# A hybrid diffusion layer: late adaLN vectors as weighted sums on VectorE, gates spread by a transfer through DRAM

## The chip, the cores and the metric

The kernel runs on one core of one Trainium2 chip. The metric is the device time of one execution in microseconds (us), the median over several runs. A core has TensorE (PE in the profile, its weight loads as PEld), VectorE (DVE), ScalarE (ACT), GpSimd (POOL) and SyncE (SP, which here only issues transfers), each with an instruction queue of its own that is worked off in order; they wait for each other by semaphores.

## The reference, cut to what matters

One step of one trunk layer for 128 context tokens and 512 latent tokens, D = 1024 channels. Every token is modulated by vectors computed from a condition: `c_ctx` for the context tokens, `c` for the latent ones.

```python
def adaln(cond, w_mod, b_mod):
    m = jax.nn.silu(cond) @ w_mod + b_mod            # w_mod: 1024 x 6144
    return jnp.split(m[..., None, :], 6, axis=-1)
...
sh1, sc1, g1, sh2, sc2, g2 = adaln(c, w_mod[l], b_mod[l])      # and the same with c_ctx
h = rmsnorm(xs, norm1_g[l]) * (1.0 + sc1) + sh1
y, _ = token_mixer(h, *mix_w, pos_lat, ctx)
xs = xs + g1 * y
h = rmsnorm(xs, norm2_g[l]) * (1.0 + sc2) + sh2
xs = xs + g2 * conv_ffn(h, w_up[l], conv_w[l], conv_b[l], w_down[l])
```

`token_mixer` projects `h` to queries, keys, values and gates, runs attention and a bidirectional retention, projects each branch (`w_att_o`, `w_ret_o`), merges them by sigmoid gates and projects by `w_out`. `conv_ffn` is an up projection, a width-3 convolution, a gate and a down projection. `sh1` and `sc1` are needed at the start; the change is about the other four vectors, called late here: `sc2` and `sh2`, needed ahead of the second norm, and the gates `g1` and `g2`, needed at the two residual additions. Each is 1024 numbers for each of the two conditions.

## The kernel before, in words

The 640 tokens are five tiles (NT) of 128. Products with weights are done as three fp32r products of split halves (`mm3`: high by high, high by low, low by high): a weight chunk is loaded on SP (`w_raw`, L133, two buffers), its high half is a copy on ScalarE (L144) and its low half a subtraction on VectorE (L149), eight half tiles of 128x1024 (`wh`) in turn. PE runs through its program in order:

1. The start: `sc1`, `sh1`, the first norm, keys and values, queries, attention.
2. Stage A, 261 to 327 us: 16 half-columns of `w_att_o` (`b_col`, L194 to L196: 24 products of 128x320 each, five banks). VectorE evacuates each with one instruction (L794), and after every second one a transfer on GpSimd stores the result (L796).
3. The groups, 327 to about 430 us: `a_group` over 512 columns of `w_in` for the retention's k, q and v (RK, RQ, RV), five tiles by two halves of 12 products of 128x512 (L156 to L158); the second half of the inner dimension has a weight chunk of its own, so one chunk is due every 14 to 16 us. Rotary embedding of each tile of k and q: two products on GpSimd (L840), then two instructions on VectorE (L842, L843).
4. Retention, then `w_ret_o` in units whose parts are added up by accumulating transfers (`f1.s`), then the out projection, 659 to 735 us (`wo_a`, evacuated by L1239 with the first gate), and the MLP in seven-product units, whose sums keep VectorE busy.

The late vectors are computed in fillers. `mod_rest` is a generator, advanced by one step at each `yield` of stage A (scale and shift) and of the groups (the gates). For each half vector it loads 2 MB of `w_mod` (L248), and TensorE multiplies: 8 blocks of 128 inner rows by 4 column groups, each product with the condition, 32 columns wide, as weights (L256). Four products side by side write to partitions 0, 32, 64 and 96. A copy to SBUF (L259, VectorE) and one product with a selecting constant (L264) turn the row into columns, channel by partition, and `put_vec` adds the bias.

A gate is used along the free dimension, so `gate_rows` spreads it again to all 128 partitions: for each condition and half four f32 products of the column, broadcast, with the identity (L274) and a copy on ScalarE (L276). That happens ahead of the fourth tile of the out projection's first half, and again between the out projection and the first MLP group.

Which instruction of one engine stands before which is decided when the program is built; the lists below show it.

## Time and profile before

| | |
|---|---|
| median of 3 runs | 1170.83 us (1170.36 to 1171.75) |
| profiled execution: span from first to last instruction | 1169.8 us; its own time isn't given apart from the span |
| granted TensorE clock in it | 0.998 |
| PE busy | 1143.2 us, 98% |
| PE weight loads | 1030.1 us, 88% |
| VectorE busy | 772.8 us, 66% |
| ScalarE busy | 591.5 us, 51% |
| GpSimd busy | 180.8 us, 15% |
| transfers | 145.85 MB, mean 125 GB/s |

A row of the timeline gives start and duration in us, engine, line, operation, the tile written, the tiles read, the shape, a count, and in brackets how long the engine was idle before and who released it. Products on PE overlap, so what one costs is the distance between starts, not the duration. In the names of tiles the last number only counts; `mm3.mm` and `aux3.aux` are PSUM banks, `weights.wh` split weights, `weights.raw` loaded ones.

### The profile page before, as it was taken

How to read it: one execution, taken by the hardware profiler on the slowest of the kernel's cores; microseconds unless marked ns; L12 is line 12 of the kernel's file. 1: busy time of each engine (PE TensorE's matmuls, PEld its weight loads, DVE VectorE, ACT ScalarE, POOL GpSimd, SP SyncE). 2: the span in 40 equal slices, each digit the busy share in tenths (PEclk: the TensorE clock that was granted, in tenths of full speed). 3: DMA queues.
4: the chain of work that ended last, by engine and by line, in shares of the span. 5: the costliest groups of instructions: out<-in, count | busy, mean ns of one | idle time of the engine just before them, and what ended most of it. 6: DMA issues, size and time to landing. Idle time of an engine off the chain costs nothing.

```text
span 1169.8 us, 18399 instructions
## 1 busy us (share of the span) xinstructions
PE 1143.2 (98%) x7269; PEld 1030.1 (88%) x7269; DVE 772.8 (66%) x1433; ACT 591.5 (51%) x1087; POOL 180.8 (15%) x194
## 2 busy tenths in 40 slices
PE   5999999999999999999999999999999999999996
PEld 4788899999988888888999988999899999899995
DVE  4666977765233526463757739969767688588888
ACT  5355656552132325452435526667657466565463
POOL 0042200000012200033002123002112111121012
PEclk9999999999999999999999999999999999999999
DMA  9742111116754522111217976445666657566543
GB/s 306 244 136 72 38 36 37 37 35 217 261 175 171 176 76 76 37 37 36 71 38 148 267 110 200 110 83 124 153 132 134 143 136 168 127 117 153 136 110 125
DMA packets 135848, 145.85 MB, mean 125 GB/s; under 512 B 26561, under 2 KB 101393, under 8 KB 135761
## 3 DMA queue, kind: packets, MB, share of 16 engines
q1 hardware_dynamic: 106576, 113.49, 30.1%
...
q14 instruction: 31, 0.25, 0.1%
...
## 4 chain that ended last, share of the span: by engine, by line
PE 80%; DVE 8%; ACT 5%; issue 3%; DMA 2%; POOL 1%; ACTq 0%; DVEq 0%; POOLq 0%
DMA f1.s.11_5326<-spill.u2.2_2889 1%; DMA f1.s.13_5328<-spill.u2.2_2889 1%; DVE x1.u1.1_6460 L1440 1%; DMA weights.raw.414_10840<-in_w_down 0%; POOL f0.s.5_3528 L955 0%; DMA const.u2.2_72<-in_b_mod 0%; DVE x1.u1.1_6460 L1489 0%; DVE x1.u1.1_6460 L1452 0%; ACT acts.u1.1_91 L1104 0%; DVE gt.gt0.5_7309 L1388 0%; DVE weights.raw.395_10492 L1537 0%; DVE x1.u1.1_6460 L1447 0%; DVE acts.u2.2_92 L414 0%; PE mm1.mm.11_295 L158 0%; PE mm7.mm.42_9455 L1559 0%
## 5 line engine op out<-in xcount | busy, mean ns | idle before, releaser
L796 POOL DMA_DIRECT2D spill.u2.2_2889<-f1.s.1_1161 x1 | 0.6, 588 | 130.2 <-DVE mod.u4.4_2848 L587 130.2
L1573 DVE TENSOR_TENSOR t7.u4.4_6978<-t7.u4.4_6978,const.u1.1_70 128x322 f32<-128x322 f32 x10 | 5.0, 496 | 11.8 <-ACT const.u1.1_70 L1572 11.8
L1085 POOL DMA_DIRECT2D weights.wh.164_5980<-weights.raw.156_5913 x1 | 1.3, 1347 | 69.6 <-DVE f1.s.9_5324 L1125 69.6
L892 DVE SCALAR_TENSOR_TENSOR ret2.u1.1_4325<-ret2.u1.1_4325,const.u13.13_88 64x128 f32<-64x128 f32 x24 | 6.8, 339 | 6.6 <-ACT ret2.u1.1_4325 L885 6.5
L894 DVE SCALAR_TENSOR_TENSOR ret2.u1.1_4325<-ret2.u1.1_4325,const.u13.13_88 64x128 f32<-64x128 f32 x24 | 6.6, 386 | 4.8 <-ACT ret2.u1.1_4325 L887 4.8
L842 DVE TENSOR_TENSOR ret.u5.5_3531<-ret.u5.5_3531,ret.u1.1_3524 128x512 f32<-128x512 f32 x5 | 3.5, 692 | 9.4 <-POOL ret.r2k.8_3709 L840 3.3
L842 DVE TENSOR_TENSOR ret.u4.4_3530<-ret.u4.4_3530,ret.u1.1_3524 128x512 f32<-128x512 f32 x5 | 3.5, 692 | 9.0 <-POOL ret.r2k.11_3889 L840 4.7
L566 POOL TENSOR_TENSOR p1.u1.1_605<-p1.u3.3_609,p1q.u1.1_599 128x512 f32<-128x512 f32 x1 | 1.3, 1310 | 43.9 <-DMA p1.u4.4_611<-in_cache_k 43.9
L149 DVE TENSOR_TENSOR weights.wh.108_4359<-weights.raw.106_4356,weights.wh.107_4358 128x1024 fp32r<-128x1024 f32 x1 | 1.2, 1224 | 10.3 <-ACT weights.wh.107_4358 L144 10.3
L144 ACT CAST weights.wh.112_4514<-weights.raw.111_4512 128x1024 fp32r<-128x1024 f32 x1 | 1.1, 1050 | 13.2 <-PE mm3.mm.36_4223 L157 13.2
L411 ACT CAST acts.u1.1_91<-f0.s.2_105 128x640 fp32r<-128x640 f32 x4 | 2.9, 728 | 9.5 <-DVE f0.s.2_105 L409 9.5
L259 DVE COPY mod2.wr.9_4315<-aux3.aux.15_4282 128x128 f32<-128x128 f32 x1 | 0.3, 291 | 10.9 <-PE aux3.aux.15_4282 L256 10.9
L428 PE MATMUL aux1.aux.1_135<-const.u1.1_70,const.u2.2_72 80*128 80x80 f32 x1 | 0.4, 365 | 7.0 <-DMA const.u2.2_72<-in_b_mod 7.0
L955 POOL TENSOR_TENSOR f0.s.5_3528<-f0.s.5_3528,ret2.ny20.13_4911 128x512 f32<-128x512 f32 x5 | 6.0, 1236 | 8.0 <-DVE ret2.ny20.13_4911 L219 8.0
L535 ACT ACTIVATE f0.s.3_711<-f0.s.3_711,p1q.ny20.11_879 128x128 f32<-128x128 f32 x20 | 6.0, 388 | 2.5 <-DVE p1q.ny20.11_879 L217 2.5
L144 ACT CAST weights.wh.67_3362<-weights.raw.66_3360 128x1024 fp32r<-128x1024 f32 x1 | 1.0, 1045 | 11.5 <-PE mm3.mm.8_3141 L195 11.5
L144 ACT CAST weights.wh.77_3617<-weights.raw.76_3615 128x1024 fp32r<-128x1024 f32 x1 | 1.0, 1045 | 11.5 <-PE mm3.mm.16_3454 L195 11.5
L144 ACT CAST weights.wh.72_3542<-weights.raw.71_3540 128x1024 fp32r<-128x1024 f32 x1 | 1.0, 1045 | 11.4 <-PE mm3.mm.12_3298 L195 11.4
L1451 DVE TENSOR_TENSOR x1.u1.1_6460<-x1.u1.1_6460,gate.u1.1_6447 128x512 f32<-128x512 f32 x10 | 6.8, 686 | 0.0
L144 ACT CAST weights.wh.92_3979<-weights.raw.91_3977 128x1024 fp32r<-128x1024 f32 x1 | 1.0, 1047 | 11.2 <-PE mm3.mm.26_3760 L157 11.2
L861 POOL MEMSET ret2.u2.2_4326<- 128x512 f32 x1 | 0.5, 525 | 38.9 <-PE aux3.aux.15_4282 L256 38.9
L1484 POOL TENSOR_TENSOR x1.u1.1_6460<-x1.u1.1_6460,weights.raw.422_11041 128x512 f32<-128x512 f32 x3 | 4.9, 1649 | 10.2 <-ACT x1.tm.112_11054 L1457 7.4
...
## 6 DMA issues: line engine op xcount, KB each, us to landing
spill.u1.1_2888<-x1.u1.1_6460 POOLq DMA_DIRECT2D x5, 512.0 KB, 3.6
xin.u1.1_103<-in_x_sample SPq DMA_DIRECT2D x4, 512.0 KB, 4.7
p0.u5.5_120<-in_w_mod SPq DMA_DIRECT2D x2, 1024.0 KB, 10.2
p0.u6.6_126<-in_w_mod SPq DMA_DIRECT2D x2, 1024.0 KB, 15.2
p0.u7.7_129<-in_w_mod SPq DMA_DIRECT2D x2, 1024.0 KB, 12.1
mod.wm.6_2916<-in_w_mod SPq DMA_DIRECT2D x1, 2048.0 KB
mod.wm.8_3069<-in_w_mod SPq DMA_DIRECT2D x1, 2048.0 KB, 8.5
mod.wm.10_3226<-in_w_mod SPq DMA_DIRECT2D x1, 2048.0 KB, 8.7
```

What stands on the lines that cost most here:

```text
L144: nc.scalar.copy(hi, rv)
L411: nc.scalar.copy(hT[0][:, k, :], xk)
L535: nc.scalar.activation(x[:, j], x[:, j], AF.Copy, scale=rstd[:, j:j + 1])
L566: nc.gpsimd.tensor_mul(ct, r2[:, :, 0, :], gqk[:, i:i + 1, :].to_broadcast([P, 4, P]))
L842: V.tensor_mul(z, z, r1[:, t, 0:1, :].to_broadcast([P, 8, 64]))
L892: V.scalar_tensor_tensor(Ss[0:64, hh, st + 1, j], Ss[0:64, hh, st, j], cdsel[0:64, h:h + 1], Ss[0:64, hh, st + 1, j], op0=ALU.mult, op1=AL ...
L894: V.scalar_tensor_tensor(Ss[64:128, hh, 2 - st, j], Ss[64:128, hh, 3 - st, j], cdsel[64:128, h:h + 1], Ss[64:128, hh, 2 - st, j], op0=ALU. ...
L955: nc.gpsimd.tensor_mul(ov, ov, rso[:, 4 * t:4 * t + 4].unsqueeze(2).to_broadcast([P, 4, P]))
L1440: V.tensor_add(x1[:, t, gs], x1[:, t, gs], down_mul(ps, t, c0))
L1451: V.tensor_mul(x1[:, t, gs], x1[:, t, gs], gb[:, t == 0, gs])
L1484: eng.tensor_mul(x, x, fg[:, c0:c0 + 512])
L1573: V.tensor_sub(u[1][:, hi_u], u[1][:, hi_u], u3[i])
```

## The change

The products of the condition with `w_mod` leave PE. The four late vectors now go through one generator that runs through stage A and the groups. For each vector it loads 8 row blocks of 128x1024 (512 KB each, three buffers); for each block and condition, VectorE adds the block times the condition's number of that row, a scalar by partition, to an accumulator of 128x1024 (the first block's sum is a scaled copy on ScalarE). What is left, the sum over the 128 partitions, is one `fold` for each vector: four f32 products of 512 columns with ones as weights, 32 columns wide, one for each column group. The row goes to SBUF on ScalarE; scale and shift then become columns by four small products, two halves at once. A gate's bias is added before the fold by two accumulating transfers onto partition 0 of the accumulator; its row is halved, stored to DRAM (`gd`), and later loaded with one transfer that repeats it to all partitions (`gate_load`, 1 MB), so that `gate_rows` is gone, with the vectors `gvec`. The generator is advanced at two of three yields of stage A, and once or twice at each of the groups' yields. Of the diff, an unused helper that goes and the old `gate_rows`, printed above, are left out.

```diff
+    def put_vec(kind, i, pv):
+        def parts(x):
+            return x.rearrange("p (h q) c -> p h q c", h=2)
+
+        k4 = [P, 2, 4, 2]
+        bias = cv[:, {"sc": 8, "sh": 7}[kind], :].rearrange("p (h q) -> p h q", h=2).unsqueeze(3).to_broadcast(k4)
+        dst = parts((avec if kind == "sc" else shvec)[i])
         V.tensor_add(dst, pv, bias)
         if kind == "sc":
-            V.scalar_tensor_tensor(dst, dst, 1.0, cv[:, 2 + i, k0:k0 + 4].unsqueeze(2).to_broadcast([P, 4, 2]),
+            V.scalar_tensor_tensor(dst, dst, 1.0, cv[:, 2 + i, :].rearrange("p (h q) -> p h q", h=2).unsqueeze(3).to_broadcast(k4),
                                    op0=ALU.add, op1=ALU.mult)
 
...
+    def gate_load(i, dst):
+        nc.sync.dma_start(dst.rearrange("p c n -> p (c n)"), gd[i:i + 1, :].to_broadcast([P, 2 * DM]))
+
     def mod_rest(lst, pool, aux):
-        s128 = cond_tile(pool)
-        V.tensor_copy(s128[:, :, 0:2], s32)
-        late = None
-        for kind, i, col in lst:
-            for n in range(2):
-                w = pool([P, KD, 512], tag="wm", bufs=1)
-                c0 = col + 512 * n
-                nc.sync.dma_start(w, a["w_mod"][0, :, c0:c0 + 512].rearrange("(k p) n -> p k n", p=P))
-                for step in range(6):
-                    yield
-                    if step == 0 and late:
-                        late()
-                ps = aux([P, 512], tag="aux")
-                for k in range(KD):
-                    for j in range(4):
-                        nc.tensor.matmul(ps[32 * j:32 * j + 32, :P], s128[:, k, :], w[:, k, j * P:(j + 1) * P],
-                                         start=k == 0, stop=k == KD - 1)
-                row = pool([P, P], tag="wr", bufs=1)
-                V.tensor_copy(row, ps[:, :P])
+        ones = pool([P, 32])
+        nc.gpsimd.memset(ones, 1.0)
+        steps = [(v, k) for v in range(len(lst)) for k in range(KD)]
+        ws, accs = [], {}
+
+        def load():
+            if len(ws) < len(steps):
+                v, k = steps[len(ws)]
+                w = pool([P, DM], tag="wm", bufs=3)
+                nc.sync.dma_start(w, a["w_mod"][0, k * P:(k + 1) * P, lst[v][2]:lst[v][2] + DM])
+                ws.append(w)
+
+        def fold(v):
+            kind, i, _ = lst[v]
+            ps = aux([P, 512], tag="aux")
+            for j in range(4):
+                nc.tensor.matmul(ps[32 * j:32 * j + 32, :], ones, accs[v][:, j // 2, (j % 2) * 512:(j % 2 + 1) * 512],
+                                 start=True, stop=True)
+            row = pool([P, 512], tag="wr", bufs=1)
+            nc.scalar.activation(row, ps, AF.Copy, scale=0.5 if kind == "g" else 1.0)
+            if kind == "g":
+                nc.gpsimd.dma_start(gd[i].rearrange("(j n) -> j n", j=4), row[::32, :])
+                return None
+            return lambda: vec(kind, i, row)
+
+        def vec(kind, i, row):
+            pv = aux([P, 512], tag="aux")
+            for q in range(4):
+                nc.tensor.matmul(pv[:, 4 * q:4 * q + 4], row[:, q * P:(q + 1) * P], cst[:, C_SEL:C_SEL + 8:2],
+                                 start=True, stop=True)
+            put_vec(kind, i, pv[:, :16].rearrange("p (q c h) -> p h q c", q=4, c=2))
+
+        for _ in range(2):
+            load()
+        later = {}
+        for n, (v, k) in enumerate(steps):
+            if k == 0:
+                accs[v] = pool([P, 2, DM], tag="acc", bufs=2)
+            for c in range(2):
                 yield
-
-                def late(row=row, kind=kind, i=i, n=n):
-                    pv = aux([P, 512], tag="aux")
-                    nc.tensor.matmul(pv[:, :8], row, cst[:, C_SEL:C_SEL + 8], start=True, stop=True)
-                    put_vec(kind, i, 4 * n, pv[:, :8].rearrange("p (j c) -> p j c", c=2))
-                yield
-        late()
-
...
+                d, sc = accs[v][:, c], s32[:, k, c:c + 1]
+                if k == 0:
+                    nc.scalar.activation(d, ws[n], AF.Copy, scale=sc)
+                else:
+                    V.scalar_tensor_tensor(d, ws[n], sc, d, op0=ALU.mult, op1=ALU.add)
+                if (n, c) in later:
+                    later.pop((n, c))()
+            load()
+            if k == KD - 1:
+                if lst[v][0] == "g":
+                    col = 2048 + 3072 * lst[v][1]
+                    for c in range(2):
+                        nc.gpsimd.dma_start(accs[v][0:1, c, :], a["b_mod"][0:1, col:col + DM], accum_op=ALU.add)
+
+                def folds(v=v, n=n):
+                    f = fold(v)
+                    if f:
+                        later[n + 2, 0] = f
+                later[n + 1, 1] = folds
+        for key in sorted(later):
+            yield
+            yield
+            later.pop(key)()
 
...
-    ada = mod_rest((("sc", 1, 4096), ("sh", 1, 3072)), mp, aux)
+    modp = Pool("mod")
+    ada = mod_rest((("sc", 1, 4096), ("sh", 1, 3072), ("g", 0, 2048), ("g", 1, 5120)), modp, aux)
 
     dp = Pool("spill", space=bass.MemoryType.DRAM)
     x1d = dp([P, NT, DM])
     thd = dp([P, KD, TOK])
+    gd = dp([2, 2 * DM])
 
     for c in range(KD):
         if c % 2 == 0:
@@ -794,9 +813,9 @@
             V.scalar_tensor_tensor(tha[c][:, ts], tha[c][:, ts], 1.0, ps, op0=ALU.add, op1=ALU.mult)
             if hf:
                 nc.gpsimd.dma_start(thd[:, c, :], tha[c])
-        for _ in b_col(w, cc, yaTk, mm, ya_ev):
-            next(ada, None)
-    run(ada)
+        for n, _ in enumerate(b_col(w, cc, yaTk, mm, ya_ev)):
+            if (4 * c + n) % 3 < 2:
+                next(ada, None)
     mp.close()
     yap.close()
 
...
-    mp = Pool("mod2", side="right")
-    ada = mod_rest((("g", 0, 2048), ("g", 1, 5120)), mp, aux)
-
...
     for i, (off, ev) in enumerate(((O_RK, evac_rqk(1)), (O_RQ, evac_rqk(0)), (O_RV, evac_rv(0)))):
         for j, _ in enumerate(a_group(w_in[:, off:off + 512], hTk, mm, ev)):
             next(ada, None)
+            if j % 3 == 0:
+                next(ada, None)
             if i == 2 and j < 8:
                 decay_tables(j)
     rv1 = a_group(w_in[:, O_RV + 512:O_RV + 1024], hTk, mm, evac_rv(1))
     for _ in range(4):
         next(rv1)
     run(ada)
-    mp.close()
+    modp.close()
 
...
         gb = gbp([P, 2, DM])
+        gate_load(0, gb)
...
-    for _ in range(3):
-        next(wo_a)
-    gate_rows(0, gb, aux, "aux")
...
-    gate_rows(1, gb, mm, "mm")
+    gate_load(1, gb)
 
```

In the lists of the changed kernel, lines have its own numbers: L813 is the evacuation L794, L148 the low half L149, L193 to L195 the products L194 to L196, L155 to L157 those of L156 to L158, L856, L858 and L859 the rotary products L840, L842 and L843. New are L251 (load of a row block), L286 (sum on VectorE), L284 (on ScalarE), L258 (fold), L270 (products to columns), L294 (bias), L263 (store of a gate's row) and L239 (`gate_load`).

VectorE in the second half of stage A, before: evacuations (`f1.s` from a bank), low halves, and between them the copy of a row and the vector's two instructions.

```order
L794 SCALAR_TENSOR_TENSOR f1.s.5_1165<-f1.s.5_1165,mm3.mm.9_3213 128x320
L230 TENSOR_TENSOR const.u8.8_83<-aux3.aux.4_3241,const.u3.3_78 128x8
L232 SCALAR_TENSOR_TENSOR const.u8.8_83<-const.u8.8_83,const.u3.3_78 128x8
L794 SCALAR_TENSOR_TENSOR f1.s.5_1165<-f1.s.5_1165,mm3.mm.10_3245 128x320
L794 SCALAR_TENSOR_TENSOR f1.s.6_1166<-f1.s.6_1166,mm3.mm.11_3272 128x320
L149 TENSOR_TENSOR weights.wh.73_3543<-weights.raw.71_3540,weights.wh.72_3542 128x1024
L259 COPY mod.wr.11_3344<-aux3.aux.5_3311 128x128
L794 SCALAR_TENSOR_TENSOR f1.s.6_1166<-f1.s.6_1166,mm3.mm.12_3298 128x320
L149 TENSOR_TENSOR weights.wh.75_3547<-weights.raw.71_3540,weights.wh.74_3546 128x1024
```

The same engine at the same place now (`mod.acc` is an accumulator, `mod.wm` a row block):

```order
L286 SCALAR_TENSOR_TENSOR mod.acc.13_3302<-mod.wm.15_3352,const.u4.4_79,mod.acc.13_3302 128x1024 x2
L813 SCALAR_TENSOR_TENSOR f1.s.6_1164<-f1.s.6_1164,mm3.mm.11_3219 128x320
L286 SCALAR_TENSOR_TENSOR mod.acc.13_3302<-mod.wm.16_3402,const.u4.4_79,mod.acc.13_3302 128x1024
L148 TENSOR_TENSOR weights.wh.73_3440<-weights.raw.71_3437,weights.wh.72_3439 128x1024
L813 SCALAR_TENSOR_TENSOR f1.s.6_1164<-f1.s.6_1164,mm3.mm.12_3248 128x320
L286 SCALAR_TENSOR_TENSOR mod.acc.13_3302<-mod.wm.16_3402,const.u4.4_79,mod.acc.13_3302 128x1024
L148 TENSOR_TENSOR weights.wh.75_3444<-weights.raw.71_3437,weights.wh.74_3443 128x1024
L286 SCALAR_TENSOR_TENSOR mod.acc.13_3302<-mod.wm.17_3460,const.u4.4_79,mod.acc.13_3302 128x1024
L813 SCALAR_TENSOR_TENSOR f1.s.7_1165<-f1.s.7_1165,mm3.mm.13_3286 128x320
L286 SCALAR_TENSOR_TENSOR mod.acc.13_3302<-mod.wm.17_3460,const.u4.4_79,mod.acc.13_3302 128x1024
```

Sums stand between any two evacuations and low halves, and each must be done before what is behind it.

VectorE in the first group, before: the low halves of a chunk, then the rotary instructions tile by tile.

```order
L149 TENSOR_TENSOR weights.wh.83_3764<-weights.raw.81_3761,weights.wh.82_3763 128x1024
L149 TENSOR_TENSOR weights.wh.85_3768<-weights.raw.81_3761,weights.wh.84_3767 128x1024
L842 TENSOR_TENSOR ret.u5.5_3531<-ret.u5.5_3531,ret.u1.1_3524 128x512
L843 TENSOR_TENSOR ret.u5.5_3531<-ret.u5.5_3531,ret.r2k.6_3638 128x512
L842 TENSOR_TENSOR ret.u5.5_3531<-ret.u5.5_3531,ret.u1.1_3524 128x512
```

Now, the last rows up to the low half of the chunk after it:

```order
L858 TENSOR_TENSOR ret.u5.5_3431<-ret.u5.5_3431,ret.u1.1_3424 128x512
L286 SCALAR_TENSOR_TENSOR mod.acc.23_3594<-mod.wm.30_3787,const.u4.4_79,mod.acc.23_3594 128x1024
L859 TENSOR_TENSOR ret.u5.5_3431<-ret.u5.5_3431,ret.r2k.7_3564 128x512
L858 TENSOR_TENSOR ret.u5.5_3431<-ret.u5.5_3431,ret.u1.1_3424 128x512
L286 SCALAR_TENSOR_TENSOR mod.acc.23_3594<-mod.wm.30_3787,const.u4.4_79,mod.acc.23_3594 128x1024
L859 TENSOR_TENSOR ret.u5.5_3431<-ret.u5.5_3431,ret.r2k.8_3586 128x512
L858 TENSOR_TENSOR ret.u5.5_3431<-ret.u5.5_3431,ret.u1.1_3424 128x512
L837 TENSOR_TENSOR ret.u2.2_3426<-ret.u2.2_3426,const.u1.1_70 128x128
L859 TENSOR_TENSOR ret.u5.5_3431<-ret.u5.5_3431,ret.r2k.9_3608 128x512
L148 TENSOR_TENSOR weights.wh.88_3742<-weights.raw.86_3739,weights.wh.87_3741 128x1024
```

Rotary instructions, which wait for GpSimd, and sums alternate, and the low half `wh.88` stands behind them all.

On PE, one fold of four products stands where two blocks of 32 did; the first comes between the 14th and the 15th half-column. PE ahead of the out projection's fourth tile (`mm.78`), before:

```order
L158 MATMUL mm3.mm.77_6475<-weights.wh.186_6354,acts.u2.2_92 128x512
L274 MATMUL aux3.aux.87_6514<-const.u1.1_70,const.u5.5_80 128x128 x4
L274 MATMUL aux3.aux.88_6520<-const.u1.1_70,const.u5.5_80 128x128 x4
L274 MATMUL aux3.aux.89_6526<-const.u1.1_70,const.u5.5_80 128x128 x4
L274 MATMUL aux3.aux.90_6532<-const.u1.1_70,const.u5.5_80 128x128 x4
L156 MATMUL mm3.mm.78_6476<-weights.wh.184_6324,acts.u1.1_91 128x512
```

Now, `mm.77` is followed by `mm.78`; what stands in place of the products is on SP, ahead of the residual rows:

```order
L132 DMA weights.raw.189_6288<-in_w_out 128x4x512
L239 DMA gate.u1.1_6295<-spill.u3.3_2891 128x2048
L1249 DMA x1.u1.1_6309<-in_x_prompt 128x1024
L1249 DMA x1.u1.1_6309<-in_x_sample 128x1024 x4
L132 DMA weights.raw.198_6480<-in_w_out 128x4x512
```

The gate's load stands ahead of the five loads of x that the out projection's evacuation also reads.

27 lines of the change are left out of this document (removed).

## The prediction

> **What bounds the kernel now.** I read the page first (busy shares, slices, the chain that ended last), then the busy time by stage, then single instructions. From the page:
>
> ```profile
> PE 1143.2 (98%) x7269; PEld 1030.1 (88%) x7269; DVE 772.8 (66%) x1433; ACT 591.5 (51%) x1087; POOL 180.8 (15%) x194
> PE   5999999999999999999999999999999999999996
> PE 80%; DVE 8%; ACT 5%; issue 3%; DMA 2%; POOL 1%; ACTq 0%; DVEq 0%; POOLq 0%
> ```
>
> TensorE (PE) is busy in every slice but the ends, and 80% of the chain is its own work: a microsecond off PE is a microsecond off the time unless something else becomes late. So I sum PE, then ask stage by stage what becomes late. The stages that the change touches (columns: PE, weight loads, VectorE, ScalarE, GpSimd, clock, DMA share, GB/s):
>
> ```profile
> 261.00:333.00 72.00, 72.00 (x677) 69.14 (x676) 33.26 (x85) 19.05 (x36) 4.39 (x8) 1.00 0.66 235
> 333.00:362.00 29.00, 29.00 (x183) 23.63 (x183) 11.69 (x16) 7.03 (x9) 8.54 (x10) 1.00 0.49 169
> 362.00:391.00 29.00, 29.00 (x183) 23.68 (x182) 12.40 (x18) 8.80 (x15) 7.93 (x10) 1.00 0.41 145
> 735.00:767.00 32.00, 31.76 (x204) 31.57 (x203) 31.51 (x30) 19.73 (x28) 1.70 (x2) 1.00 0.43 105
> ```
>
> PE never pauses from 261 to 391 at full clock, and VectorE (DVE) is less than half busy there: that is the room for the sums. From 735 to 767 DVE is as full as PE.
>
> **What is removed, all on PE.** One of the eight blocks of 32 small products (L256) inside a half-column of stage A, and one of the eight 128x8 products (L264):
>
> ```profile
> 273.62 0.31 PE L196 MATMUL mm3.mm.4_2984<-ya.u1.1_2824,weights.wh.53_2893 128*128 128x320 f32 x1
> 273.86 1.95 PE L256 MATMUL aux3.aux.1_2997<-mod.wm.6_2916,mod.s128.5_2913 128*32 128x128 f32 x64
> ...
> 276.00 0.31 PE L195 MATMUL mm3.mm.4_2984<-ya.u2.2_2825,weights.wh.54_2896 128*128 128x320 f32 x1
> 276.15 0.31 PE L196 MATMUL mm3.mm.4_2984<-ya.u1.1_2824,weights.wh.55_2897 128*128 128x320 f32 x1
> ...
> 281.00 0.31 PE L196 MATMUL mm3.mm.5_3056<-ya.u1.1_2824,weights.wh.60_3053 128*128 128x320 f32 x1
> 281.14 0.28 PE L264 MATMUL aux3.aux.2_3084<-const.u1.1_70,mod.wr.7_3030 128*128 128x8 f32 x2
> ...
> 281.51 0.31 PE L195 MATMUL mm3.mm.6_3088<-ya.u2.2_2825,weights.wh.57_3048 128*128 128x320 f32 x1
> 281.66 0.31 PE L196 MATMUL mm3.mm.6_3088<-ya.u1.1_2824,weights.wh.58_3049 128*128 128x320 f32 x1
> ```
>
> Starts are read, not durations, since products overlap. Undisturbed ones follow at 0.15 us (276.00 to 276.15; more exactly 0.147 over many). From 273.62 to 276.15 are 2.53 us with three such steps in them: the block costs 2.53 - 0.44 = 2.09. From 281.00 to 281.66 are 0.66: the small product costs 0.22. Eight of each: 16.7 + 1.8 = 18.5 us.
>
> The gate spreading (L274), before the fourth tile of the out projection and before the MLP's group:
>
> ```profile
> 667.18 1.05 PE L274 MATMUL aux3.aux.87_6514<-const.u1.1_70,const.u5.5_80 128*128 128x128 f32 x8
> ...
> 670.23 1.16 PE L274 MATMUL aux3.aux.90_6532<-const.u1.1_70,const.u5.5_80 128*128 128x128 f32 x8 [0.21 <-ACT gate.u1.1_6447 L276]
> 671.14 0.48 PE L156 MATMUL mm3.mm.78_6476<-weights.wh.184_6324,acts.u1.1_91 128*128 128x512 f32 x1
> 671.46 0.40 PE L157 MATMUL mm3.mm.78_6476<-weights.wh.185_6325,acts.u1.1_91 128*128 128x512 f32 x1
> ...
> 751.44 1.05 PE L274 MATMUL mm7.mm.1_7285<-const.u1.1_70,const.u6.6_81 128*128 128x128 f32 x8
> ...
> 755.41 0.42 PE L1336 MATMUL mm7.mm.5_7371<-acts.u1.1_91,weights.wh.211_7345 128*128 128x322 f32 x1 [0.24 <-ACT gate.u1.1_6447 L276]
> 755.66 0.31 PE L1337 MATMUL mm7.mm.5_7371<-acts.u2.2_92,weights.wh.211_7345 128*128 128x322 f32 x1
> ```
>
> 667.18 to 671.14 and the slower step after it (0.32 against 0.23) are 4.05 us; 751.44 to 755.41 and its step (0.25 against 0.15) are 4.07. Both hold waits for ScalarE's copies, which go too. Removed in all: 18.5 + 8.1 = **26.6 us**.
>
> **What is added on PE.** Four folds (L258) of four 32x512 f32 products, one for each column group. In the block above 64 records run in 1.95 us; a group's share is 8 products of 128 columns, 1024 columns in about 1.88, so the four groups run side by side. A fold is 512 columns a group: 0.94, with the block's overhead (2.09 - 1.88 = 0.21) 1.15. If the groups ran one after another, 2048 columns at the same rate would be 3.8, 4.0 with overhead. I take 1.15, since the same groups with the same type stand in the row: 4.6 us for four (upper end 16). For each scale and shift four 128x4 products (L270), at L264's 0.22: 8 x 0.22 = 1.8. Net on PE: -26.6 + 4.6 + 1.8 = **-20.2 us**.
>
> **What is added elsewhere.** 56 sums on DVE (L286) and 8 on ScalarE (L284), 128x1024 each. The nearest rows:
>
> ```profile
> 759.08 1.49 DVE L1393 SCALAR_TENSOR_TENSOR gt.gt0.5_7309<-gt.gt1.6_7310,acts.u1.1_91 128x1288 f32<-128x1288 f32 x1
> 760.49 0.82 DVE L1362 TENSOR_TENSOR gt.gt1.8_7326<-x1.row.57_7261,gt.gt0.7_7325 128x641 fp32r<-128x641 f32 x1
> ...
> 357.79 1.22 DVE L149 TENSOR_TENSOR weights.wh.88_3869<-weights.raw.86_3866,weights.wh.87_3868 128x1024 fp32r<-128x1024 f32 x1
> ...
> 359.00 1.69 DVE L149 TENSOR_TENSOR weights.wh.90_3873<-weights.raw.86_3866,weights.wh.89_3872 128x1024 fp32r<-128x1024 f32 x1
> ...
> 344.57 1.43 POOL L840 TENSOR_TENSOR ret.r2k.6_3638<-ret.u5.5_3531,ret.u1.1_3524 128x256 f32<-128x256 f32 x2 [16.23 <-ACT ret.u5.5_3531 L836]
> ...
> 358.46 2.82 POOL L840 TENSOR_TENSOR ret.r2k.10_3747<-ret.u5.5_3531,ret.u1.1_3524 128x256 f32<-128x256 f32 x2 [2.04 <-ACT ret.u5.5_3531 L836]
> ```
>
> The same operation with 1288 columns takes DVE for 1.41 us (759.08 to 760.49); 1024 columns scale to 1.12, and a two-input pass over 1024 is 1.21 from 357.79 to 359.00. I take 1.15, so 56 x 1.15 = 64 us on DVE. 28 of them stand ahead of stage A's last evacuation in DVE's order: 33 + 32 = 65 us of DVE work in a stage that PE now finishes in about 72 - 4 x 2.09 - 4 x 0.22 + 2 = 64. DVE is full there and some us behind PE at the end. PE doesn't feel it: an evacuation (L813) may be four half-columns of 24 x 0.147 = 3.5 us late, with five banks. Then 27 sums stand from the split of chunk wh.80 to that of wh.98, 31 us, beside some 24 us of old work over 333 to 391: 55 us in the 57 to 62 that PE gives. What PE next needs from DVE are the low halves of the weights, in DVE's queue behind those sums:
>
> ```profile
> 388.11 1.22 DVE L149 TENSOR_TENSOR weights.wh.98_4122<-weights.raw.96_4119,weights.wh.97_4121 128x1024 fp32r<-128x1024 f32 x1
> ...
> 403.36 0.40 PE L157 MATMUL mm3.mm.27_3972<-weights.wh.98_4122,acts.u1.1_91 128*128 128x512 f32 x1
> ```
>
> A low half is done 14.0 us ahead of its first product here (389.33 against 403.36). Walking DVE's new order with these durations, wh.83, wh.88, wh.93 and wh.98 come 7 to 10 us ahead: the slack shrinks, and PE waits for nothing. The folds ask for sums that ended 10 us or more before. Shorter waits I count with 0.3 us (a product of L270 that follows its fold's copy too closely).
>
> Against that stands the last pair of rows. Two GpSimd products (L840) need 1.43 us alone and 2.82 beside L149, and that L149 1.69 instead of 1.22. Both engines read two operands from SBUF, and neither ran through the other. Ten rope tiles lie among the sums: DVE loses 0.47 for each as in this row, 4.7 us, or the whole 1.43, 14.3 us. Against a slack of about 10 at wh.98 that is 0 to 4 us of PE waiting; I put 1.0 into the sum.
>
> [...]
>
> **Loads.** 16 MB of w_mod as before, now 32 pieces of 512 KB in three buffers.
>
> ```profile
> xin.u1.1_103<-in_x_sample SPq DMA_DIRECT2D x4, 512.0 KB, 4.7
> mod.wm.8_3069<-in_w_mod SPq DMA_DIRECT2D x1, 2048.0 KB, 8.5
> weights.raw.86_3866<-in_w_in SPq DMA_DIRECT2D x1, 1024.0 KB, 9.3
> ```
>
> A piece lands in some 4.7 us (5 to 9 at worst, by the 1 MB row). With its two sums (2.3) and a wait to issue (0.5), three buffers give one piece in (4.7 + 2.3 + 0.5) / 3 = 2.5 us; the pace that DVE can take is 2.3 and that the code asks for in the groups is about 3.3. So DVE is the tighter one. The raw loads queue behind these on SP, still early. GpSimd gets two adding transfers for each gate (L294) between rope tiles, about 0.6 us of issue each: no one waits.
>
> **The gates.** Around the first one:
>
> ```profile
> 657.33 8.19 DMA f1.s.13_5328<-spill.u2.2_2889
> ...
> 659.74 0.34 SPq L1230 DMA_DIRECT2D x1.u1.1_6460<-in_x_prompt  x1
> ...
> 669.93 1.22 DVE L149 TENSOR_TENSOR weights.wh.193_6453<-weights.raw.188_6438,weights.wh.192_6452 128x1024 fp32r<-128x1024 f32 x1
> ...
> 676.81 0.40 PE L156 MATMUL mm3.mm.75_6473<-weights.wh.190_6448,acts.u1.1_91 128*128 128x512 f32 x1
> ...
> 679.80 0.69 DVE L1239 TENSOR_TENSOR x1.tm.4_6574<-mm3.mm.75_6473,gate.u1.1_6447 128x512 f32<-128x512 f32 x1 [0.71 <-PE mm3.mm.75_6473 L158]
> ```
>
> Its load (L239) goes out on SP where x1's first row does, at 659.74, waiting for the row in DRAM, written long before; it lands in 5 to 9 us and is needed first by L1239, 4 us sooner than 679.80: in time. PE's second half starts 4.05 us sooner, at 672.8, and DVE's last low half for it ends at 671.15, behind an accumulating transfer that ends at 665.52 and now has the gate's 1 MB beside it. 1.6 us of room: nothing lost, at most some 2. For the second:
>
> ```profile
> 765.10 0.82 DVE L1362 TENSOR_TENSOR gt.gt1.8_7326<-x1.row.59_7269,gt.gt0.7_7325 128x641 fp32r<-128x641 f32 x1
> ...
> 769.83 0.39 PE L156 MATMUL acc7.acc.1_7502<-weights.wh.216_7357,gt.gt0.7_7325 128*128 128x512 f32 x1
> ```
>
> PE's down products wait for what DVE, full since 735, finishes at 765.92. PE was 3.9 us later than that and comes 4.07 earlier: 0.2 us of the gain is lost at once, 2 if DVE's chain slips a little. I take 0.5. Behind it PE is continuous again, so gains last to the end.
>
> **The sum.** -20.2 + 0.3 + 1.0 + 0.5 = -18.4 us. The profiled execution's span is 1169.8 us, and the runs' median, 1170.83, lies 1.0 above it: 1151.4 as a span, **1152.4 us** as a time. A change under 0.2% (2.3 us) can't be told from none.
>
> **Rivals.**
> 1. DVE becomes the bound in the groups: the full 1.43 at each rope tile (4 us), and pieces that land in 7 us instead of 4.7 (0.8 us more for each of the 13 to 14 pieces there, 10 us of slip, most of it beyond the slack). PE waits 3 to 11 us: 1155 to 1163. For it: DVE has hardly an idle microsecond; against: 14 us of slack now. Chance 0.22.
> 2. The folds don't run side by side: + 4 x 2.85 = 11.4, 1164. For it: products of 512 columns in this form stand nowhere in the trace. Chance 0.06.
> 3. The second gate's 4 us are lost in DVE's full stretch: 1156. For it: 31.51 of 32 us; against: the 3.9 us. Chance 0.10.
> 4. Slower than before: the pieces come so late that DVE, held in order by an L286 that waits, holds back the low halves. To undo the 18.4 us and the slack of 10, the 21 pieces after stage A must take 28 us more than their 70, 4.7 us each, so 11.3 us to land 512 KB in three buffers. The slowest 2 MB row took 10.3. Chance 0.04; price at 12 us: 1176.
> 5. Better than forecast: DVE never makes PE wait and the gates cost nothing, 1149 to 1150.5. Chance 0.10, beside 0.48 for the forecast (1150.5 to 1155).
>
> Range 1149 to 1163: it leaves out the serial folds, the slower case and some of the edges, under 2 in 10. Faster 0.94, within 0.2% 0.02, slower 0.04.
>
> **What would show it.** Folds: four products starting within 0.1 us and done in about 1.2. Sums: L286 at 1.12 to 1.25 us, more beside L856 of GpSimd (L840 now). PE: no wait over 0.3 us before wh.78's products, and none named for L148's low halves from 319 to 405. Gates: PE goes from the third tile straight on; the first L1239 doesn't wait for gate. I am wrong if PE waits in the groups for DVE, or if a fold lasts over 2 us.

## The result, and the profile after

| | before | after |
|---|---|---|
| median of the runs | 1170.67 us (1170.36 to 1171.75, 4 runs) | 1159.03 us (1157.72 to 1161.30, 4 runs) |
| profiled execution: span | 1169.8 us | 1155.9 us (its time: 1157.72 us) |
| granted TensorE clock in it | 0.998 | 0.998 |

The ratio is 0.9901, 95% interval 0.9888 to 0.9913: faster by 11.6 us where 18.4 were forecast. The time lies inside the range of 1149 to 1163, but outside the forecast's own band (1150.5 to 1155) and among the times of its first rival (1155 to 1163), so the sum has an error of some 7 us to be found. By the two profiled spans the gain is 13.9 us.

The page after, the lines of busy time, of PE's slices and of the chain:

```profile
PE 1125.0 (97%) x6725; PEld 1010.4 (87%) x6725; DVE 840.2 (73%) x1466; ACT 597.6 (52%) x1091; POOL 193.4 (17%) x201
PE   5999999999999999999999998999999999999996
PE 78%; DVE 10%; DMA 4%; issue 4%; ACT 3%; POOL 1%; ACTq 0%; DVEq 0%; SPq 0%; POOLq 0%
```

PE lost 18.2 us of busy time (1143.2 before), and one slice in the middle fell under 90%: that is the first hint of a wait that was not there. In the chain DMA went from 2% to 4% and DVE from 8% to 10%. What PE waited for, in the list of waits of the kernel after (us in total, times, longest):

```profile
PE mm3.mm.87_6905 L1354 <- DMA weights.wh.208_6823<-weights.raw.204_6815: 3.2, 1, 3.2
...
PE mm3.mm.27_3855 L156 <- DVE weights.wh.98_3991 L148: 1.2, 1, 1.2
PE mm3.mm.27_3855 L156 <- DVE weights.wh.93_3863 L148: 0.6, 1, 0.6
```

None of these three is in the list of before. Two are the low halves that the prediction priced at 1.0; the third, a weight of the MLP at 719 us, stands nowhere in it. The stages of the sums after (columns: PE, weight loads, VectorE, ScalarE, GpSimd, clock, DMA share, GB/s):

```profile
261.00:319.00 58.00, 58.00 (x397) 56.76 (x397) 54.02 (x89) 17.12 (x24) 3.86 (x7) 1.00 0.77 257
...
348.00:377.00 29.00, 29.00 (x134) 23.22 (x134) 28.81 (x29) 9.23 (x12) 14.20 (x12) 1.00 0.54 179
377.00:394.00 17.00, 16.38 (x73) 11.83 (x71) 16.97 (x16) 3.60 (x8) 5.01 (x7) 1.00 0.27 87
```

VectorE is full from 348 on, and PE stays at work until 377: the stage has just run out of VectorE's slack at its end.

### The profile page after: what moved, and what is told of

It reads as the page before. It is cut to its first block, busy times and chain, and to the rows that moved or that the text cites. A ratio compares the mean times of both kernels' runs of the same rounds, so it can differ in the third digit from the quotient of the medians.

```text
span 1155.9 us, 17421 instructions
## 1 busy us (share of the span) xinstructions
PE 1125.0 (97%) x6725; PEld 1010.4 (87%) x6725; DVE 840.2 (73%) x1466; ACT 597.6 (52%) x1091; POOL 193.4 (17%) x201
## 4 chain that ended last, share of the span: by engine, by line
PE 78%; DVE 10%; DMA 4%; issue 4%; ACT 3%; POOL 1%; ACTq 0%; DVEq 0%; SPq 0%; POOLq 0%
DMA weights.wh.208_6823<-weights.raw.204_6815 1%; DVE mod.acc.23_3594 L286 1%; DVE mod.acc.13_3302 L286 1%; DMA mod.wm.27_3693<-in_w_mod 1%; DVE x1.u1.1_6309 L1456 1%; DMA mod.wm.36_3914<-in_w_mod 1%; DVE mod.acc.33_3853 L286 1%; DMA weights.raw.414_10642<-in_w_down 0%; DMA mod.wm.21_3570<-in_w_mod 0%; DMA weights.wh.410_10583<-weights.raw.397_10313 0%; POOL f0.s.5_3428 L973 0%; DVE ret.u4.4_3430 L858 0%; DMA const.u2.2_72<-in_b_mod 0%; DVE x1.u1.1_6309 L1505 0%; DMA mod.wm.39_4033<-in_w_mod 0%
## 5 line engine op out<-in xcount | busy, mean ns | idle before, releaser
L910 DVE SCALAR_TENSOR_TENSOR ret2.u1.1_4173<-ret2.u1.1_4173,const.u11.11_86 64x128 f32<-64x128 f32 x24 | 6.8, 338 | 6.6 <-ACT ret2.u1.1_4173 L903 6.5
L148 DVE TENSOR_TENSOR weights.wh.113_4363<-weights.raw.111_4360,weights.wh.112_4362 128x1024 fp32r<-128x1024 f32 x1 | 1.2, 1226 | 12.5 <-ACT weights.wh.112_4362 L143 12.5
L912 DVE SCALAR_TENSOR_TENSOR ret2.u1.1_4173<-ret2.u1.1_4173,const.u11.11_86 64x128 f32<-64x128 f32 x24 | 6.6, 381 | 4.8 <-ACT ret2.u1.1_4173 L905 4.8
L428 ACT CAST acts.u1.1_89<-f0.s.2_103 128x640 fp32r<-128x640 f32 x4 | 2.9, 727 | 9.5 <-DVE f0.s.2_103 L426 9.5
L552 ACT ACTIVATE f0.s.3_709<-f0.s.3_709,p1q.ny20.11_877 128x128 f32<-128x128 f32 x20 | 6.0, 387 | 2.5 <-DVE p1q.ny20.11_877 L216 2.5
L428 ACT CAST acts.u1.1_89<-f0.s.1_102 128x640 fp32r<-128x640 f32 x4 | 2.9, 727 | 8.2 <-DVE f0.s.1_102 L426 8.2
L284 ACT ACTIVATE mod.acc.23_3594<-mod.wm.21_3570,const.u4.4_79 128x1024 f32<-128x1024 f32 x2 | 2.3, 1151 | 9.2 <-DMA mod.wm.21_3570<-in_w_mod 9.2
L143 ACT CAST weights.wh.67_3278<-weights.raw.66_3276 128x1024 fp32r<-128x1024 f32 x1 | 1.1, 1054 | 11.3 <-PE mm3.mm.8_3121 L194 11.3
L552 ACT ACTIVATE p1.u4.4_609<-p1.u4.4_609,p1.ny10.15_659 128x128 f32<-128x128 f32 x10 | 3.0, 389 | 6.4 <-DVE p1.ny10.15_659 L216 6.4
L261 ACT ACTIVATE mod.wr.41_4166<-aux3.aux.6_4161 128x512 f32<-128x512 f32 x1 | 0.6, 600 | 10.9 <-issue 10.9
L552 ACT ACTIVATE f0.s.4_958<-f0.s.4_958,p1q.ny20.20_1126 128x128 f32<-128x128 f32 x20 | 6.2, 399 | 0.0
```

The costliest lines, as they stand in the source:

```text
L284: nc.scalar.activation(d, ws[n], AF.Copy, scale=sc)
L428: nc.scalar.copy(hT[0][:, k, :], xk)
L552: nc.scalar.activation(x[:, j], x[:, j], AF.Copy, scale=rstd[:, j:j + 1])
L910: V.scalar_tensor_tensor(Ss[0:64, hh, st + 1, j], Ss[0:64, hh, st, j], cdsel[0:64, h:h + 1], Ss[0:64, hh, st + 1, j], op0=ALU.mult, op1=AL ...
L912: V.scalar_tensor_tensor(Ss[64:128, hh, 2 - st, j], Ss[64:128, hh, 3 - st, j], cdsel[64:128, h:h + 1], Ss[64:128, hh, 2 - st, j], op0=ALU. ...
```

## The experiments

Two theories for the three waits. A: the second gate's load of 1 MB meets the accumulating transfer that builds the low half `wh.208`, and makes it late. C: GpSimd's rotary products and VectorE's two-input instructions take turns, so that VectorE falls behind with `wh.93` and `wh.98`. The rival to both is that VectorE or the queues are simply full, so that moving one thing makes another late. Each experiment's time stands beside runs of the kernel before on the same chip (1171.07 us for the first four, 1171.23 us for the second four).

**1. The second gate's load later.** It goes out behind step 24 (counted from 0) of the MLP's loop, after a copy that ties it there; its rows are first used at 1059.7 us in the kernel after.

```diff
-    gate_load(1, gb)
...
+            if n == 24:
+                V.tensor_copy(gb[0:1, 0, 0:1], x1[0:1, 0, 0:1])
+                gate_load(1, gb)
```

> The second gate's load (1 MB) is held back by a one-element copy on VectorE until well into the MLP; nothing else moves. Theory A, the load slows the accumulating transfers of the up projection's low halves, for which PE waits 3.15 us at wh.208: the transfer of wh.208 takes about 7 us instead of 10.9, the wait falls to 0.5 us or less, the span falls by 3 us to about 1153. Rival B, PE only comes too early there, since the first gate's products no longer hold it up, or the 512 KB stores of x1 slow the transfers: the transfer still takes 10 to 11 us, the wait stays at 3 us, the span at 1156 to 1159.

Measured: 1155.22 us (1154.17 to 1156.18), ratio 0.9864, interval 0.9848 to 0.9881. The transfer's rows in the list of issues (KB, us to landing), first after, then with the load later:

```profile
gate.u1.1_6295<-spill.u3.3_2891 SPq DMA_DIRECT2D x1, 1024.0 KB, 7.5
weights.wh.208_6823<-weights.raw.204_6815 POOLq DMA_DIRECT2D x1, 512.0 KB, 10.9
```

```profile
weights.wh.208_6823<-weights.raw.204_6815 POOLq DMA_DIRECT2D x1, 512.0 KB, 7.0
```

And the timeline after, with the gate's load, the load that stands behind it on SP, the issue of `wh.208` and PE's first product with it:

```profile
707.99 0.34 SPq L239 DMA_DIRECT2D gate.u1.1_6295<-spill.u3.3_2891  x1
...
708.43 1.20 SPq L1466 DMA_DIRECT2D x1.tm.94_10152<-spill.u1.1_2889  x1
...
708.55 1.34 POOL L146 DMA_DIRECT2D weights.wh.208_6823<-weights.raw.204_6815  x1 [0.43 <-ACT weights.wh.208_6823 L145]
...
719.51 0.39 PE L1354 MATMUL mm3.mm.87_6905<-acts.u1.1_89,weights.wh.208_6823 128*128 128x256 f32 x1 [3.15 <-DMA weights.wh.208_6823<-weights.raw.204_6815]
```

The same in the timeline with the load later:

```profile
703.41 0.34 SPq L1465 DMA_DIRECT2D x1.tm.94_10153<-spill.u1.1_2889  x1
...
708.83 1.35 POOL L146 DMA_DIRECT2D weights.wh.208_6823<-weights.raw.204_6815  x1 [0.44 <-ACT weights.wh.208_6823 L145]
...
709.01 0.34 SPq L1465 DMA_DIRECT2D x1.tm.95_10171<-spill.u1.1_2889  x1
...
710.16 0.32 SPq L1465 DMA_DIRECT2D x1.tm.97_10211<-spill.u1.1_2889  x1
...
716.49 0.28 PE L1354 MATMUL mm3.mm.87_6905<-acts.u1.1_89,weights.wh.208_6823 128*128 128x256 f32 x1
```

PE needs the low half 7.7 us after its transfer is issued (708.83 to 716.49). With the gate's load moved, the transfer takes 7.0; with the gate's megabyte on the way since half a microsecond, 10.9. The wait is gone with the load, and theory A holds, with an addition: the expectation says that nothing else moves, but the loads behind the gate's in SP's queue do. `x1.tm.94`, 256 KB, goes out at 703.41 without the gate's load and lands 3.8 us later, ahead of the transfer; with it, it goes out at 708.43, beside the transfer. The next two, 256 KB each, go out beside the transfer without the gate's load (709.01 and 710.16), and with it only after PE's wait (720.08 and 721.35). So the transfer of 10.9 us met loads of 1.25 MB, and that of 7.0 loads of 0.5 MB; what the gate's own megabyte does, and what its place in SP's queue does, isn't told apart here.

By the spans this run gains 2.4 us, less than the wait, because the wait at `wh.93` is 1.5 us here and 0.6 in the kernel after, though the edit doesn't touch it. The kernel before shows how thin the margin at `wh.208` was:

```profile
721.91 1.34 POOL L147 DMA_DIRECT2D weights.wh.208_6998<-weights.raw.204_6990  x1 [0.43 <-ACT weights.wh.208_6998 L146]
...
729.57 0.28 PE L1338 MATMUL mm3.mm.87_7080<-acts.u1.1_91,weights.wh.208_6998 128*128 128x256 f32 x1
```

There too the product comes 7.7 us after the issue, and the transfer took 7.0: a margin of some 0.7 us that no row quoted in the prediction shows.

**2. The rotary products on VectorE.** The two products of each rotary tile move from GpSimd, so that nothing of GpSimd's runs beside the sums but transfers' issues.

```diff
-                nc.gpsimd.tensor_mul(sw[:, :, b * 32:(b + 1) * 32], xs,
+                V.tensor_mul(sw[:, :, b * 32:(b + 1) * 32], xs,
```

> The two rotary products of each tile (L856) run on VectorE instead of GpSimd. Theory C, the two engines take turns at operands in SBUF: VectorE loses about 12 us to GpSimd now and pays some 20 x 0.35 = 7 us for the products itself, so the low halves come earlier: the waits of 0.8 us at wh.93 and 1.35 us at wh.98 shrink to nothing, L286 always takes 1.27 us. Rival D, VectorE is simply full and GpSimd costs it nothing: 7 us more work on it make the waits 7 us longer, the span about 1163.

Measured: 1156.25 us (1155.15 to 1157.58), ratio 0.9874, interval 0.9859 to 0.9888. The kernel after, VectorE and GpSimd around 375 and 387 us:

```profile
373.47 1.76 DVE L286 SCALAR_TENSOR_TENSOR mod.acc.33_3853<-mod.wm.37_3956,const.u4.4_79,mod.acc.33_3853 128x1024 f32<-128x1024 f32 x1
375.15 1.76 DVE L286 SCALAR_TENSOR_TENSOR mod.acc.33_3853<-mod.wm.38_3979,const.u4.4_79,mod.acc.33_3853 128x1024 f32<-128x1024 f32 x1
376.83 1.75 DVE L148 TENSOR_TENSOR weights.wh.93_3863<-weights.raw.91_3860,weights.wh.92_3862 128x1024 fp32r<-128x1024 f32 x1
...
380.84 1.27 DVE L286 SCALAR_TENSOR_TENSOR mod.acc.33_3853<-mod.wm.39_4033,const.u4.4_79,mod.acc.33_3853 128x1024 f32<-128x1024 f32 x1
382.04 0.68 DVE L858 TENSOR_TENSOR ret.u4.4_3430<-ret.u4.4_3430,ret.u1.1_3424 128x512 f32<-128x512 f32 x1
...
387.44 2.73 DVE L286 SCALAR_TENSOR_TENSOR mod.acc.33_3853<-mod.wm.40_4057,const.u4.4_79,mod.acc.33_3853 128x1024 f32<-128x1024 f32 x1
...
390.70 2.58 DVE L858 TENSOR_TENSOR ret.u4.4_3430<-ret.u4.4_3430,ret.u1.1_3424 128x512 f32<-128x512 f32 x1
...
393.92 1.22 DVE L148 TENSOR_TENSOR weights.wh.98_3991<-weights.raw.96_3988,weights.wh.97_3990 128x1024 fp32r<-128x1024 f32 x1
```

```profile
374.10 3.40 POOL L856 TENSOR_TENSOR ret.r2k.13_3803<-ret.u4.4_3430,ret.u1.1_3424 128x256 f32<-128x256 f32 x2
...
387.36 1.73 POOL L856 TENSOR_TENSOR ret.r2k.14_3824<-ret.u4.4_3430,ret.u1.1_3424 128x256 f32<-128x256 f32 x2
```

While GpSimd works, sums follow at 1.68 us (373.47 to 375.15) and GpSimd's products take 1.70 each; when it has stopped, a sum lasts 1.27 and the next instruction follows after 1.20 (380.84 to 382.04). Each product of GpSimd so costs VectorE 0.48 us, and where it gets a pair in at one go, 1.46 (2.73 instead of 1.27). With the rotary products on VectorE, one row of its list of L286 (duration in ns, least, median, most):

```profile
L286 DVE SCALAR_TENSOR_TENSOR mod.acc.33_3853<-mod.wm.38_3979,const.u4.4_79,mod.acc.33_3853 x2: 1276/1276/1277, 374.2 to 376.7; 128x1024 f32<-128x1024 f32 x2
```

and its two rows in the timeline that matter, the low half and PE's product:

```profile
387.96 1.22 DVE L148 TENSOR_TENSOR weights.wh.98_3991<-weights.raw.96_3988,weights.wh.97_3990 128x1024 fp32r<-128x1024 f32 x1
...
391.83 0.40 PE L156 MATMUL mm3.mm.27_3855<-weights.wh.98_3991,acts.u1.1_89 128*128 128x512 f32 x1
```

VectorE does the 20 products itself, 6.7 us of it, and is done with `wh.98` 6.0 us earlier (389.2 against 395.1), 2.6 us ahead of PE. Part of this is order: three sums, 3.6 us, now stand behind that low half, and ten small decay instructions of 0.2 us and a tile's last two rotary instructions, 3.2 us in all, ahead of it. The rest is the turns. Added up over 319 to 395 us by the distance between starts, without VectorE's idle time, the 30 sums took 42.8 us after and 36.0 here, nine L858 9.3 against 5.4 at 0.60 each, and three low halves 0.55 more each: some 12 us. Theory C holds for VectorE's time; the next experiment asks whether the turns are what PE's waits need. The wait at `wh.208` stays here, 2.6 us.

**3. A slower pace.** The generator's extra step in every third step of the projections is left out, so that fewer sums stand ahead of `wh.93` and `wh.98`; GpSimd keeps its products.

```diff
-            if j % 3 == 0:
-                next(ada, None)
```

> The extra step of the generator at every third yield of the groups goes, so 6 of the 14 sums ahead of wh.98 move behind it, into the third group. If the waits for wh.93 and wh.98 come from sums in front of them, both go and the span falls by 2 us to about 1154, unless the last sums now hold up what follows the groups. If the waits come from late weight loads instead, they stay and the span is as the changed kernel's.

Measured: 1156.83 us (1155.67 to 1157.42), ratio 0.9877, interval 0.9862 to 0.9892. Neither `wh.93` nor `wh.98` is in the list of waits; the wait at `wh.208` stays, 2.2 us.

```profile
386.01 1.21 DVE L148 TENSOR_TENSOR weights.wh.98_3960<-weights.raw.96_3957,weights.wh.97_3959 128x1024 fp32r<-128x1024 f32 x1
...
391.26 0.40 PE L156 MATMUL mm3.mm.27_3836<-weights.wh.98_3960,acts.u1.1_89 128*128 128x512 f32 x1
```

`wh.98` starts on VectorE at 386.01 us and PE's product comes at 391.26 without a wait, though sums beside GpSimd still follow at 1.67 to 1.69 us. So it is not the turns in themselves that cost time, but VectorE's being late at two places, and a means that puts the low halves earlier in its queue does as well.

The traces show one more thing that makes VectorE late: it idles for a piece of `w_mod`, which took 7.1 us to land where the prediction had 4.7. In the kernel after:

```profile
336.48 2.96 DVE L286 SCALAR_TENSOR_TENSOR mod.acc.23_3594<-mod.wm.27_3693,const.u4.4_79,mod.acc.23_3594 128x1024 f32<-128x1024 f32 x2 [1.45 <-DMA mod.wm.27_3693<-in_w_mod]
```

At this place experiments 1 to 5 idle 1.2 to 1.9 us. The wait at `wh.93` goes with it: 0.6 us where VectorE idled 1.45 us (after) and 1.32 (experiment 4), 1.5 us where it idled 1.66 (experiment 1) and 1.90 (experiment 5). Experiments 2 and 3 have this idle time too, and no wait at `wh.93`, so the late piece alone doesn't make PE wait; what it adds to the turns was not tried by itself.

**4. and 5. The sums alone: gates still spread by PE.** The folded row of a gate becomes columns by the products of L270 as for scale and shift, and `gate_rows` stands as before. In the first of the two the columns' product comes two steps after the fold, in the second six.

```diff
-    def gate_load(i, dst):
-        nc.sync.dma_start(dst.rearrange("p c n -> p (c n)"), gd[i:i + 1, :].to_broadcast([P, 2 * DM]))
+    def gate_rows(i, dst, pool, tag):
...
-                        later[n + 2, 0] = f
+                        later[n + (6 if lst[v][0] == "g" else 2), 0] = f
```

> The gates are spread on PE as before (gate rows, two products' groups each; the gate's row goes to columns by four small products first); the sums stay on VectorE. PE gets back 8.1 us and 1.8 us for the columns. Theory A: the wait at wh.208 goes with the load (3.3 us), so the span grows by 6.6 us to about 1162.5. Rival B: PE also comes later to wh.208 (4 us), so the wait goes too, and this run doesn't tell A from B; a rival in which the wait stays gives 1166. The gates' part of the gain is this difference.

Measured: 1180.20 us (1179.67 to 1182.19), ratio 1.0081, interval 1.0066 to 1.0096, slower than before, which no theory had. ScalarE and PE in its timeline:

```profile
378.49 0.39 ACT L842 ACTIVATE ret.r2k.17_3923<-const.u1.1_70,const.u11.11_86 128x128 f32<-128x128 f32 x1
383.70 0.40 ACT L842 ACTIVATE ret.r2k.18_3943<-const.u1.1_70,const.u11.11_86 128x128 f32<-128x128 f32 x1 [4.82 <-DVE ret.u4.4_3431 L865]
...
396.80 0.40 ACT L842 ACTIVATE ret.r2k.22_4043<-const.u1.1_70,const.u11.11_86 128x128 f32<-128x128 f32 x1 [3.28 <-DVE ret.u4.4_3431 L865]
397.10 0.58 ACT L271 ACTIVATE mod.wr.34_3889<-aux3.aux.5_3884 128x512 f32<-128x512 f32 x1
```

```profile
397.74 1.87 PE L277 MATMUL aux3.aux.6_3894<-const.u1.1_70,mod.wr.34_3889 128*128 128x4 f32 x8 [15.06 <-ACT mod.wr.34_3889 L271]
```

The copy of the folded row stands on ScalarE behind decay activations (L842), which wait for VectorE to free a buffer (4.82 and 3.28 us in these rows), and VectorE is full, 14.97 of 15 us from 382 to 397. PE in its turn waits for the copy: 15 us. In the kernel after a gate's row leaves by a transfer, and PE asks for nothing. The fifth run moves the product away from this:

> The version with the sums on VectorE but the gates still spread by PE, with the gates' columns product six steps behind instead of two. Theory: the 15 us PE stall of the earlier version came because this product waits for a ScalarE copy that is queued behind decay activations, which wait for VectorE; four more steps of projection products lie ahead of it now, so the stall is gone, and the time is that of the sums alone: from the kernel before, 1170.7 - 18.5 (sums and their column products on PE) + 4.8 (folds) + 3.6 (four vectors' column products) + 2.1 (low halves) = 1162.7 us; from the changed kernel, 1159.0 + 8.1 (gate rows) + 1.8 (two column products) - 3.2 (no load beside wh.208) = 1165.7 us. So 1162 to 1166, with no wait at wh.208. Rival: the stall is only moved, and the time stays over 1172 us.

Measured: 1163.35 us (1162.74 to 1165.25), ratio 0.9937, interval 0.9922 to 0.9951. The 15 us are gone, there is no wait at `wh.208`, and the low halves of `wh.93` and `wh.98` cost 1.5 and 1.2 us. The sums alone bring 7.9 us.

**6. The gates alone.** The late vectors are products on PE as before, spread at the changed kernel's pace, and only the gates go through DRAM. This kernel leaves out the gates' bias, so it says something of the time alone.

```diff
-                    V.scalar_tensor_tensor(d, ws[n], sc, d, op0=ALU.mult, op1=ALU.add)
+                        nc.tensor.matmul(ps[32 * j:32 * j + 32, :P], s128[:, k, :], w[:, k, j * P:(j + 1) * P],
+                                         start=k == 0, stop=k == KD - 1)
...
+                        nc.gpsimd.dma_start(gd[i][c * DM + 512 * n:c * DM + 512 * n + 512].rearrange("(j p) -> j p", j=4), row[c::32, :])
```

> The other part alone: the later vectors' sums are products on TensorE as in the kernel before, and only the gates go through DRAM (the gates' bias is left out). Theory: from the kernel before, 1170.7 - 8.1 (gate rows) - 0.9 (gates' column products) + 3.2 (the second gate's load beside wh.208's accumulating transfer) = 1164.9 us; from the changed kernel, 1159.0 + 17.6 (sums and column products) - 4.8 (folds) - 1.8 (column products) - 2.1 (low halves in time again) = 1167.9 us. So 1164.5 to 1168, with the wait at wh.208 of 2.3 to 3.3 us still there and none at wh.93 and wh.98. Rival: the late wh.208 needs the later time at which PE gets there with the sums on VectorE, then no wait there and 1161.7 us.

Measured: 1167.72 us (1165.34 to 1169.42), ratio 0.9969, interval 0.9959 to 0.9980. The wait at `wh.208` is there (2.9 us) with the sums on PE, so it doesn't need them on VectorE, and the rival with 1161.7 falls; that it needs the load, and not only the absence of the gate's products, is experiment 1. The gates alone bring 3.5 us, the sums alone 7.9, together 11.4 against 11.6 for the whole change: within their intervals, some 1.2 and 1.7 us to either side, the parts add up.

**7. and 8. Both waits mended.** The later load together with the rotary products on VectorE, and together with the slower pace.

> Two edits to the changed kernel together: the second gate's load moved behind the 24th step of the MLP loop, and the rope products on VectorE instead of GpSimd. Theory: the two waits are independent (3.2 us for wh.208's accumulating transfer at 716 us, 2.1 us or a little more for the low halves of wh.93 and wh.98 around 380 us), so the gains add: against the changed kernel's 1159.0 us, 3.8 us (measured alone: 1155.2) and 2.8 us (1156.3) give 1152.5 us, 1151.5 to 1153.5, with no PE wait over 1 us between 200 and 1100 us. Rival: both only shift when PE reaches a later fixed point (the retention stage or the MLP's weights), so the second gains nothing: 1155.2 us.

> The second gate's load moved, and the extra step of the sums in every third step of the projections left out (slower pace); the rope products stay on GpSimd. Theory: the slower pace alone gained 2.2 us (1156.8 against 1159.0), the load alone 3.8 us, so together 1153.0 us, 1152.0 to 1154.0, within 1 us of the version with the rope products on VectorE: what counts is that VectorE isn't late with the low halves at 378 and 395 us, by whichever means. Rival: the turns with GpSimd cost more than those two waits, and this version is over 1.5 us slower than the one with the rope on VectorE.

Measured: 1153.09 us (1152.04 to 1154.21), ratio 0.9846, interval 0.9832 to 0.9861, and 1151.90 us (1151.38 to 1153.20), ratio 0.9838, interval 0.9823 to 0.9852, 0.1 us under its expected range. Of the first, the list of waits has of the three only

```profile
PE mm3.mm.87_6905 L1354 <- DMA weights.wh.208_6823<-weights.raw.204_6815: 0.3, 1, 0.3
```

and of the second none. The gains add within the runs' spread, and nothing else makes PE wait over 0.4 us between 200 and 1100 us; the two versions can't be told apart, since their intervals overlap. Either is faster than before and after; the second is the best measured here, 1.6% under the kernel before.

## Why the prediction was right, and where it was off

By the profiled spans:

| term | forecast, us | measured, us | from |
|---|---|---|---|
| blocks, small products and gate rows removed from PE | -26.6 | -26.6 (taken over) | not measured by itself; the check is experiment 8, below |
| four folds | +4.6 | +4.8 | 1.20 each |
| columns' products | +1.8 | +1.8 | 0.90 for four |
| shorter waits | +0.3 | +0.3 | |
| low halves late | +1.0 | +2.1 | experiments 2 and 3 |
| second gate, VectorE's full stretch | +0.5 | 0 | no wait at the down products |
| second gate's load beside `wh.208` | none | +3.3 | experiments 1 and 6 |
| sum | -18.4 | -14.3 | spans: -13.9 |

Two steps of the prediction failed: the term for the low halves was too small by about half, and the second gate's load had no term at all. By its own sign, PE waiting in the groups for VectorE, the forecast was wrong there. That the time still lies in the range is partly luck: it falls among the first rival's times, but VectorE's lateness made 2.1 us of waits where that rival had 3 to 11, and the larger wait stands in no case.

**PE's own terms were right.** The second fold in the timeline after:

```profile
347.56 0.40 PE L157 MATMUL mm3.mm.21_3436<-weights.wh.79_3528,acts.u2.2_90 128*128 128x512 f32 x1
347.89 1.06 PE L258 MATMUL aux3.aux.3_3633<-mod.acc.13_3302,mod.u1.1_2915 128*32 128x512 f32 x8
348.89 0.50 PE L155 MATMUL mm3.mm.22_3649<-weights.wh.82_3656,acts.u1.1_89 128*128 128x512 f32 x1
349.23 0.40 PE L156 MATMUL mm3.mm.22_3649<-weights.wh.83_3657,acts.u1.1_89 128*128 128x512 f32 x1
```

From 347.56 to 349.23 are 1.67 us with two steps of 0.23 in them, so a fold costs 1.20 where the prediction took 1.15 from a block of other shape in the same column groups; the serial rival (4.0) falls. The best test of PE's terms together is experiment 8, where none of the three waits is left: its span is 1150.1 us, 19.7 under the span of before, and the prediction's terms without those waits are -20.2 + 0.3 = -19.9.

**The low halves: right mechanism, size off.** The prediction walked VectorE's order and found `wh.83` to `wh.98` 7 to 10 us ahead, then set 4.7 to 14.3 us of turns with GpSimd against that and put 1.0 into the sum. Measured, a sum is 1.20 instead of 1.15 (1.5 us over 30 sums), the turns cost some 12 us, near the upper end, VectorE idled 1.6 us for late pieces, and the slack is used up: 0.78 us at `wh.93` and 1.35 at `wh.98`, starts against the undisturbed pitch. The step that failed is the reading of one row of before: 0.47 us was taken as the loss for a rotary *tile*, though it is the loss for one of GpSimd's two products, and in that row only one VectorE instruction ran into GpSimd's pair. The prediction's upper figure, the whole 1.43 us of GpSimd's pair at each tile and so 14.3 in all, came nearer to VectorE's loss: the trace shows turns (a sum at 1.76 instead of 1.27, and 2.73 beside a pair) and some 12 us. For PE's wait this figure gave 4 us at `wh.98` where 1.35 were measured, 2.1 with `wh.93`. The full length of a product isn't seen at each turn: 0.48 of 0.7 us where the products alternate with VectorE's instructions, all of it where a pair gets in at one go (1.46 for the two).

**The second gate's load: the step that was missing.** The prediction looked for what the first gate's load meets, found 1.6 us of room there, and nothing was lost. For the second gate it looked at VectorE alone, and of the load's issue at 708 us it said nothing, though it moves a megabyte, and the load held up behind it, into a stretch where the accumulating transfer of `wh.208` feeds PE with some 0.7 us to spare. (The one ahead of it, `wh.206`, had 3.2 us before: 4.9 to land, 8.1 from its issue to its product.) This is the largest error, 3.3 us by the profile and 3.8 by the median time of experiment 1. The loss of 0.5 in VectorE's full stretch didn't come, and not in experiment 8 either, where PE gets there 6.8 us sooner still: no wait at the first down products is in its list.

**The rest.** The median gain, 11.6 us, is 2.3 below that of the profiled spans. Some 0.9 of this is on the side of before: the prediction took a time to lie 1.0 us above its span, but the profiled execution after took 1157.72 us for a span of 1155.9, 1.8 more, and later runs of the kernel before show the same (1171.26 for 1169.5). By this the profiled execution of before lies some 0.9 us above its median. The other 1.3 is on the side of after, where the other three runs are 0.9 to 3.6 us longer than the profiled one, at a clock of 0.996 or 0.997 instead of 0.998. A likely reason is in the last section, but those runs have no trace, so it stays open.
